# Two stages reordered in a hybrid encoder kernel: low parts behind the next modulation and h made twice by ScalarE; mask squares earlier, one small operation fewer a row, sample keys behind the masks

## Chip, cores and metric

The kernel runs on one core of one Trainium2 chip. The metric is the device time in microseconds (us) of one launch; the time before is the median of three runs. TensorE (PE) multiplies, VectorE (DVE), ScalarE (ACT) and GpSimd (POOL) work beside it, and SyncE (SP) issues the loads. All five run their own instruction lists and wait for each other by semaphores.

## What is computed

One inference step of a two-layer encoder trunk, width 1024, on 1024 prompt positions and 64 sample positions, all in float32. Each layer is `x += gate(c) * mixer(RMSNorm(x) * (1 + scale(c)) + shift(c))`. What the change touches is all in layer 0:

```python
rel = jax.nn.relu(jnp.einsum('bqhd,bsd->bqhs', qi, ki)).astype(jnp.float32)
score = jnp.einsum('bqh,bqhs->bqs', wi.astype(jnp.float32), rel)
adm = (kpos[None, :] // CHUNK) <= (qpos[:, None] // CHUNK)
score = jnp.where(adm[None], score, -jnp.inf)
top_val, top_idx = lax.top_k(score, topk)          # 256 keys of each query
...
logits = jnp.einsum('bqgrd,bqkgd->bqgrk', q, kg).astype(jnp.float32) * (HEAD_DIM ** -0.5)
logits = jnp.where(valid[:, :, None, None, :], logits, -jnp.inf)
p = jax.nn.softmax(logits, axis=-1).astype(v.dtype)
```

The mixer of layer 0 is this sparse attention beside a short gated convolution, both fed from one projection `h @ w_in`; layer 1 is a gated spatial unit. The sample positions attend to 512 cached keys beside their own 64.

## The kernel before

**Products.** A float32 product is made of three fast ones: an operand is split into a high part and a low part (the operand less its high part), and TensorE adds high by high, low by high and high by low. `ah` and `al` are the parts of the activations, `w_hi` and `w_lo` those of a weight tile. The high part is made by ScalarE; the low part by a subtraction on GpSimd (weights, line 253) or on VectorE.

**First stage (`startup`, lines 296 to 418).** The eight tiles of `x` (128 x 1088, one for each 128 of the width, called k-tiles, `kt`) are loaded and their squares summed. Modulation comes in four units `u`; each gives scale and shift of two k-tiles: 32 narrow matmuls (`ada_steps`, line 165), a VectorE copy of their sum (`ada_rows`, line 168), a TensorE transpose (line 171), and two or three small VectorE operations that write `mod` and `modA`. Then, for each k-tile, `scale(kt)` multiplies x by the root-mean-square factor on VectorE (line 339); `h(kt)` makes `hf`, the modulated tile in full float32, on GpSimd (line 345), the same values rounded to the high part `ah` on ScalarE (line 346), and `al = hf - ah` on VectorE (line 347); `part(kt)` issues the matmuls of that k-tile for the first two weight tiles (line 334): six with `ah, w_hi`, six with `ah, w_lo`, six with `al, w_hi`. There are two buffers for `hf`. The order of TensorE, VectorE, GpSimd and ScalarE in this stage is the order of the code: for u = 1 to 3 the modulation's matmuls, the first six matmuls of `part(2u-1)`, the transpose, the other twelve, then `scale` and `h` of the next two k-tiles, then all of `part(2u)`. The last two k-tiles are multiplied for one weight tile after the other. The common products of the later stages (line 261) follow.

**Masks (`masks`, lines 609 to 643).** A search finds for each query the threshold `T` of its 256th score. For each of seven rows of widths 384, 512, 640, 768, 896, 1024 and 576 the kernel then writes a 0/1 mask in which ties are broken by position: ScalarE makes the sign of score less threshold with its sum (line 632) and the square of that with its sum (line 622); VectorE makes a one-column number out of the two sums in two operations (lines 638 and 639), a running count along the row that starts from it (line 640), and a comparison (line 641); ScalarE then scales the mask into a bias (line 643). A sign operation of row j waits in the order for the square of row j-2 (`issue_after`). Here TensorE alone follows the order of the code; the lists of the other engines are set by the framework's planner, which places each instruction when its inputs are due.

**Around the masks.** While the masks are made, TensorE works through `side` steps, the matmuls of two more projections (line 278; 360 steps stand ahead of the attention, the masks are issued at step 289), and their sums are moved out by ScalarE (`q<-pj`). `sample_keys` loads the cached keys (`ckr`), splits them into `kc` (high on ScalarE, line 292; low on GpSimd, line 293) and copies 64 columns of `kp` behind them (line 782); `both_parts` makes the sample queries `qs` (lines 768 and 769). Both are issued ahead of the masks' order here: `sample_keys` before the side steps, `both_parts` at the start of `attend`. The attention begins with logits on TensorE (line 680), each read from its PSUM bank by a VectorE reduction (line 681) and then passed to ScalarE for the exponential. The second pair of logits has to wait until the reduction of an earlier one has freed its bank.

## Time and profile before

| what | us |
| --- | --- |
| runs | 1121.41 (median), 1119.2 to 1122.15 |
| the profiled execution | 1120.84 |
| its span, from the first instruction to the last | 1119.0 |
| TensorE busy in the span | 1080.0 (97%) |
| VectorE, ScalarE, GpSimd busy | 651.7, 524.2, 459.9 |

The profile is of one execution. Its page gives sums over the whole span; the trace gives each instruction with its start and length, and what ended the idle time before it. In the time-ordered view a row that stands for several instructions (x6) begins with the first and its length goes to the end of the last. In the view by stretches a row gives the ends of the stretch, its length, the busy time of TensorE, of its weight loads, of VectorE, ScalarE and GpSimd, then TensorE's granted clock as a share of full speed, the share of the DMA engines that was busy, and GB/s.

### The profile page before, as it was taken

Reading aid. Unit: us, or ns where it says so; the run is one execution under the profiler, and the core shown is the slowest. Engines: PE = TensorE matmul, PEld = TensorE weight load, DVE = VectorE, ACT = ScalarE, POOL = GpSimd, SP = SyncE. Lnnn points to the kernel's source line nnn. Section 1 sums busy time; section 2 is a strip of 40 time slices with the busy share of each in tenths; the row PEclk is TensorE's granted clock in tenths of the full one; section 3 lists DMA queues with packets and bytes.
Section 4 is the critical chain, followed back from the end, with each engine's and each line's share of the span. In section 5 each row is a group of like instructions: output and inputs, shape, how many; then the busy total and the mean of one; then the engine's idle time right before and its main releaser. Section 6 shows DMA issues by size and latency. Waiting matters only on the chain.

```text
span 1119.0 us, 18850 instructions
## 1 busy us (share of the span) xinstructions
PE 1080.0 (97%) x7255; PEld 1044.9 (93%) x7255; DVE 651.7 (58%) x1621; ACT 524.2 (47%) x1003; POOL 459.9 (41%) x479
## 2 busy tenths in 40 slices
PE   5899999999999979999999999999999999999996
PEld 4789778999999979999999999999999999999996
DVE  4710789998887687777786344311393083346134
ACT  5333588766776677667686234411221111244111
POOL 2634224346675625545375356411242101264222
PEclk9999999999999989999999999999999999999999
DMA  9754611211010210000002601111113101130012
GB/s 371 279 198 161 246 30 47 84 42 47 30 39 23 73 38 21 20 18 19 5 22 80 246 1 39 33 44 38 39 48 94 39 20 39 38 132 20 1 67 94
DMA packets 25786, 81.84 MB, mean 73 GB/s; under 512 B 3040, under 2 KB 9440, under 8 KB 23264
## 3 DMA queue, kind: packets, MB, share of 16 engines
q1 hardware_dynamic: 25696, 80.63, 20.5%
q8 instruction: 57, 0.93, 0.3%
q14 instruction: 33, 0.27, 0.1%
HBM read 74.50 MB, written 6.12 MB: 72 GB/s over the span
## 4 chain that ended last, share of the span: by engine, by line
PE 58%; DVE 2%; issue 1%; POOL 1%; ACT 1%; DMA 1%; POOLq 0%; DVEq 0%; ACTq 0%
PE pj L261 24%; PE op L261 15%; PE pj L278 7%; PE av L724 3%; PE logit_ps L680 3%; PE p_ps L706 3%; PE sgu_ps L1204 1%; DVE al L293 1%; DMA w_raw<-in_wo 1%; PE v_ps L1251 1%; POOL w_lo L253 1%; PE op L1123 0%; PE rstd L226 0%; PE sgus_ps L1207 0%; DVE x L1176 0%
## 5 line engine op out<-in xcount | busy, mean ns | idle before, releaser
L261 PE MATMUL pj<-ah,w_hi 128*128 128x364 f32 (+1 forms) x984 | 326.0, 331 | 1.0 <-ACT w_hi L252 1.0
L261 PE MATMUL pj<-al,w_hi 128*128 128x364 f32 (+1 forms) x984 | 323.8, 329 | 0.0
L261 PE MATMUL pj<-ah,w_lo 128*128 128x364 f32 (+1 forms) x984 | 323.0, 329 | 0.0
L253 POOL TENSOR_TENSOR w_lo<-w_raw,w_hi 128x1024 fp32r<-128x1024 f32 x63 | 155.7, 2472 | 322.1 <-ACT w_hi L252 319.8
L261 PEld LDWEIGHTS pj<-ah,w_hi 128*128 128x128 f32 x984 | 185.0, 188 | 2.0 <-ACT w_hi L252 1.3
L261 PEld LDWEIGHTS pj<-ah,w_lo 128*128 128x128 f32 x984 | 184.8, 188 | 0.3 <-issue 0.2
L261 PEld LDWEIGHTS pj<-al,w_hi 128*128 128x128 f32 x984 | 185.1, 188 | 0.0
L252 ACT ACTIVATE w_hi<-w_raw 128x1024 fp32r<-128x1024 f32 x68 | 71.8, 1057 | 107.8 <-PE pj L261 86.6
L545 DVE TENSOR_SCALAR_CACHE_REDUCE junk<-S,cand 128x512 bf16<-128x512 f32 (+5 forms) x142 | 119.0, 838 | 1.9
L261 PE MATMUL op<-al,w_hi 128*128 128x256 f32 (+2 forms) x344 | 112.0, 326 | 0.4 <-DVE al L293 0.4
L261 PE MATMUL op<-ah,w_hi 128*128 128x256 f32 (+2 forms) x344 | 112.2, 327 | 0.0
L261 PE MATMUL op<-ah,w_lo 128*128 128x256 f32 (+2 forms) x344 | 111.6, 326 | 0.0
L278 PE MATMUL pj<-ah,w_hi 128*128 128x364 f32 (+1 forms) x288 | 95.7, 332 | 0.0
L278 PE MATMUL pj<-ah,w_lo 128*128 128x364 f32 (+1 forms) x288 | 95.6, 332 | 0.0
L278 PE MATMUL pj<-al,w_hi 128*128 128x364 f32 (+1 forms) x288 | 95.4, 331 | 0.0
L572 ACT ACTIVATE junk<-S,cand 128x896 bf16<-128x896 f32 (+2 forms) x78 | 77.7, 996 | 29.2 <-DVE m L575 25.5
L1144 DVE SCALAR_TENSOR_TENSOR x<-op,mod,x 128x192 f32<-128x192 f32 (+2 forms) x64 | 30.2, 496 | 101.6 <-PE op L261 97.5
L687 POOL TENSOR_SCALAR S<-S,sm 128x128 f32<-128x128 f32 (+8 forms) x68 | 51.6, 763 | 73.2 <-DVE sm L686 60.5
L1152 POOL TENSOR_TENSOR acc<-acc,sq 128x448 f32<-128x448 f32 (+2 forms) x40 | 40.7, 1018 | 86.3 <-ACT sq L1150 85.5
L261 PEld LDWEIGHTS op<-al,w_hi 128*128 128x128 f32 x344 | 64.9, 189 | 2.5 <-DVE al L293 0.7
L1150 ACT ACTIVATE sq<-x 128x448 f32<-128x448 f32 (+2 forms) x42 | 21.3, 506 | 96.7 <-DVE x L1144 93.2
L261 PEld LDWEIGHTS op<-ah,w_hi 128*128 128x128 f32 x344 | 64.9, 189 | 1.7
(255 smaller groups left out, 2096.9 us busy)
## 6 DMA issues: line engine op xcount, KB each, us to landing
w_raw<-in_w SPq DMA_DIRECT2D x53, 512.0 KB, 3.4
ada<-in_ada_w SPq DMA_DIRECT2D x19, 1024.0 KB, 7.5
w_raw<-in_wo SPq DMA_DIRECT2D x16, 512.0 KB, 3.5
x<-in_x SPq DMA_DIRECT2D x8, 544.0 KB, 5.7
bo<-in_ada_w SPq DMA_DIRECT2D x4, 1024.0 KB, 6.8
x<-in_x SPq DMA_DIRECT2D x1, 1792.0 KB, 7.9
out_y<-x SPq DMA_DIRECT2D x1, 1792.0 KB, 6.6
x<-in_x SPq DMA_DIRECT2D x1, 1536.0 KB, 9.4
```

What stands on the lines that cost most here:

```text
L252: nc.scalar.activation(hi, raw, AF.Copy)
L253: (nc.gpsimd if lo_eng == "pool" else nc.vector).tensor_sub(lo, raw, hi)
L261: last = self.nc.tensor.matmul(ps, wt[:, kt, :], at[:, kt, c0:c1], start=n == 0, stop=n == len(mms) - 1)
L278: self.nc.tensor.matmul(ps, wt[:, kt, :], at[:, kt, a:b], start=kt == 0 and i == 0, stop=kt == KT - 1 and i == 2)
L545: V.tensor_scalar(junks[0][:, 0:SW[j]], self.S[:, span(j)], thr, 0.0, op0=OP.is_lt, op1=OP.add, accum_out=col(cv, j))
L572: nc.scalar.activation(junks[1][:, 0:SW[j]], self.S[:, span(j)], AF.Sign, scale=-1.0, bias=col(cand, j), accum_out=col(cv, j))
L680: nc.tensor.matmul(pt[:, 0:w], lhs, keys[i][:, t // 2, s], start=i == 0, stop=i == 1)
L687: self.lastnorm = nc.gpsimd.tensor_scalar(p, p, st[:, 3:4], 0.5, op0=OP.mult, op1=OP.mult).ins
L706: nc.tensor.transpose(pt[0:r, o:o + P], p[:, j * P:j * P + r], self.ident)
L724: self.lastav = nc.tensor.matmul(av[:, 0:m], self.vs[0:r, vbase + j, t // 2, :], part[0:r, x:x + m], start=j == 0 and i == 0, stop=(j + 1) ...
L1144: nc.vector.scalar_tensor_tensor(x[:, t, a:b], ps[:, a:b], self.mod[l][:, 16 + t, j:j + 1], x[:, t, a:b], op0=OP.mult, op1=OP.add)
L1152: nc.gpsimd.tensor_add(acc, acc, sq)
```

## The change

Three things are edited.

- In `startup`, `part` can issue one of its three kinds of matmuls alone. The `al, w_hi` matmuls of k-tile 2u-2 are issued behind the modulation transpose of unit u, and those of 2u-1 after them. `h` takes two k-tiles at once; `hf` is now made by ScalarE too, from the same inputs as `ah` (four more activations for two k-tiles, 16 in all, and as many fewer GpSimd operations). `scale(kt + 2)` stands ahead of the subtraction of `kt`.
- In `masks`, the square of row 0 comes ahead of the sign of row 1. One VectorE operation makes `(sum of signs - 0.5) * sum of squares` in place of two, and it is used by the comparison; the running count starts from the constant `kneg` and needs only the squares.
- `sample_keys` and `both_parts` are issued after the last square of the masks, and some tiles share other buffers.

```diff
@@ startup @@
-        def part(kt, ns=(0, 1), between=()):
-            for i, (wi, at) in enumerate(((0, self.ah), (1, self.ah), (0, self.al))):
-                if i == 1:
-                    for _ in between:
-                        pass
+        def part(kt, ns=(0, 1), which=(0, 1, 2)):
+            for i in which:
+                wi, at = ((0, self.ah), (1, self.ah), (0, self.al))[i]
...
-        def h(kt):
-            hf = sp.tile([P, TC], F32, tag="hf0", name="hf0", bufs=2)
-            for j, (a, b) in enumerate(((0, SEQ), (SEQ, TC))):
-                sc, sh = self.modA[0][:, kt, j:j + 1], self.mod[0][:, kt, j:j + 1]
-                nc.gpsimd.tensor_scalar(hf[:, a:b], x[kt][:, a:b], sc, sh, op0=OP.mult, op1=OP.add)
-                nc.scalar.activation(self.ah[:, kt, a:b], x[kt][:, a:b], AF.Identity, scale=sc, bias=sh)
-            nc.vector.tensor_sub(self.al[:, kt, :], hf, self.ah[:, kt, :])
+        def h(kts):
+            hfs = []
+            for kt in kts:
+                hfs.append(sp.tile([P, TC], F32, tag="hf0", name="hf0", bufs=2))
+                for out in (self.ah[:, kt, :], hfs[-1]):
+                    for j, (a, b) in enumerate(((0, SEQ), (SEQ, TC))):
+                        nc.scalar.activation(out[:, a:b], x[kt][:, a:b], AF.Identity, scale=self.modA[0][:, kt, j:j + 1],
+                                             bias=self.mod[0][:, kt, j:j + 1])
+            for kt, hf in zip(kts, hfs):
+                if kt + 2 < KT:
+                    scale(kt + 2)
+                nc.vector.tensor_sub(self.al[:, kt, :], hf, self.ah[:, kt, :])
...
             scale(1)
-            h(0)
-            scale(2)
-            h(1)
-            part(0)
+            h((0, 1))
+            part(0, which=(0, 1))
             w_split(0, 2, KT, nc.gpsimd)
             w_split(1, 2, KT, nc.vector)
-            scale(3)
...
-                part(2 * u - 1, between=steps)
-                for kt in (2 * u, 2 * u + 1):
-                    if kt + 2 < KT:
-                        scale(kt + 2)
-                    h(kt)
+                part(2 * u - 1, which=(0,))
+                for _ in steps:
+                    pass
+                part(2 * u - 1, which=(1,))
+                part(2 * u - 2, which=(2,))
+                h((2 * u, 2 * u + 1))
+                part(2 * u - 1, which=(2,))
                 if u < 3:
-                    part(2 * u)
+                    part(2 * u, which=(0, 1))
@@ masks @@
-            pool.tile([P, 2 * 512], BF, tag=t, name="cum", bufs=3) for t in ("ptl", "ptl", "ptl", "pth", "pth")]
+            pool.tile([P, 2 * 512], BF, tag=t, name="cum", bufs=3) for t in ("ptl", "pth", "pth", "pth", "ptl")]
...
-            with self.tc.issue_after(square) if j > 1 else nullcontext():
+            with self.tc.issue_after(square) if j else nullcontext():
                 A.activation(bi, sl, AF.Sign, scale=self.sgn[:, p], bias=self.T[:, p], accum_out=sums[:, 0:1])
-            if j:
-                square = squares(*rows[j - 1])
-        squares(*rows[-1])
+            if j != 1:
+                square = squares(*rows[j - (j > 0)])
+        self.masked = squares(*rows[-1])
         for n, bi, cum, p, sums in rows:
-            c = self.cv[:, p]
-            V.tensor_add(c, sums[:, 0:1], sums[:, 1:2])
-            V.tensor_scalar(c, c, 0.5, self.kneg[:, p], op0=OP.mult, op1=OP.add)
-            V.tensor_tensor_scan(cum, self.ones.to_broadcast([P, n]), cum, c, OP.add, OP.subtract)
-            V.scalar_tensor_tensor(bi, cum, 0.0, bi, op0=OP.is_gt, op1=OP.is_gt)
+            V.tensor_scalar(sums[:, 2:3], sums[:, 0:1], sums[:, 1:2], -0.5, op0=OP.add, op1=OP.mult)
+            V.tensor_tensor_scan(cum, self.ones.to_broadcast([P, n]), cum, self.kneg[:, p], OP.add, OP.subtract)
+            V.scalar_tensor_tensor(bi, cum, sums[:, 2:3], bi, op0=OP.is_gt, op1=OP.is_gt)
@@ sample_keys, attend and the calls @@
-            raw = pool.tile([P, PAST], F32, tag="pth", name="ckr", bufs=3)
+            raw = pool.tile([P, PAST], F32, tag="ptl", name="ckr", bufs=3)
...
-        for t in range(2):
-            self.both_parts(pool, t)
...
                     self.queries(ap, 0)
-                    self.sample_keys(ap)
                     for n in range(BEFORE):
                         if n == MASKS:
                             self.masks(ap)
+                            with self.tc.issue_after(self.masked):
+                                self.sample_keys(ap)
+                                for t in range(2):
+                                    self.both_parts(ap, t)
                         next(self.side)
```

The instruction lists show what this moves. In the first stage, ScalarE before, from the first k-tile's `ah` to the weights' high parts (line, operation, output<-inputs with buffer numbers, shape):

```order
L346 ACTIVATE ah_64<-x0_98,mod0_87,modA0_89 128x1024
L346 ACTIVATE ah_64<-x0_98,mod0_87,modA0_89 128x64
L346 ACTIVATE ah_64<-x1_99,mod0_87,modA0_89 128x1024
L346 ACTIVATE ah_64<-x1_99,mod0_87,modA0_89 128x64
L386 ACTIVATE w_hi_235<-w_raw_123 128x768
L386 ACTIVATE w_hi_237<-w_raw_124 128x768
```

And the same place on ScalarE after the change:

```order
L347 ACTIVATE ah_64<-x0_98,mod0_87,modA0_89 128x1024
L347 ACTIVATE ah_64<-x0_98,mod0_87,modA0_89 128x64
L347 ACTIVATE hf0_273<-x0_98,mod0_87,modA0_89 128x1024
L347 ACTIVATE hf0_273<-x0_98,mod0_87,modA0_89 128x64
L347 ACTIVATE ah_64<-x1_99,mod0_87,modA0_89 128x1024
L347 ACTIVATE ah_64<-x1_99,mod0_87,modA0_89 128x64
L347 ACTIVATE hf0_278<-x1_99,mod0_87,modA0_89 128x1024
L347 ACTIVATE hf0_278<-x1_99,mod0_87,modA0_89 128x64
L391 ACTIVATE w_hi_235<-w_raw_123 128x768
L391 ACTIVATE w_hi_237<-w_raw_124 128x768
```

Four activations of `hf` now stand ahead of the weights' high parts and between the two `ah`. VectorE in the same stretch, from the scaling of k-tile 1 to the modulation copy, before:

```order
L339 TENSOR_TENSOR x1_99<-x1_99,acc0_138 128x1088
L347 TENSOR_TENSOR al_65<-hf0_273,ah_64 128x1088
L339 TENSOR_TENSOR x2_100<-x2_100,acc0_138 128x1088
L347 TENSOR_TENSOR al_65<-hf0_280,ah_64 128x1088
L387 TENSOR_TENSOR w_lo_238<-w_raw_124,w_hi_237 128x768
L339 TENSOR_TENSOR x3_101<-x3_101,acc0_138 128x1088
L168 COPY ada_rows_342<-ada_ps_309 128x128
```

VectorE there after the change:

```order
L338 TENSOR_TENSOR x1_99<-x1_99,acc0_138 128x1088
L338 TENSOR_TENSOR x2_100<-x2_100,acc0_138 128x1088
L352 TENSOR_TENSOR al_65<-hf0_273,ah_64 128x1088
L338 TENSOR_TENSOR x3_101<-x3_101,acc0_138 128x1088
L352 TENSOR_TENSOR al_65<-hf0_278,ah_64 128x1088
L392 TENSOR_TENSOR w_lo_238<-w_raw_124,w_hi_237 128x768
L168 COPY ada_rows_336<-ada_ps_303 128x128
```

The scaling of x moved ahead of the subtractions; the copy `ada_rows`, for which TensorE's transpose waits, still stands behind both subtractions and the weights' low part. On TensorE the six `al, w_hi` matmuls of k-tile 0 left their place ahead of the modulation's matmuls for one behind the transpose, and likewise for k-tiles 2 and 4.

At the masks, ScalarE before, from the first sign to the first square and one further:

```order
L632 ACTIVATE bias,sums<-S,T,sgn 128x384
L252 ACTIVATE w_hi<-w_raw 128x1024
L894 ACTIVATE q<-pj 128x360
L632 ACTIVATE bias,sums<-S,T,sgn 128x512
L768 ACTIVATE qs<-q 64x64 x2
L292 ACTIVATE kc_3878<-ckr 128x512 x2
L622 ACTIVATE cum,sums<-bias 128x384
```

After the change, ScalarE from the first sign:

```order
L637 ACTIVATE bias,sums<-S,T,sgn 128x384
L252 ACTIVATE w_hi<-w_raw 128x1024
L896 ACTIVATE q<-pj 128x360
L627 ACTIVATE cum,sums<-bias 128x384
L637 ACTIVATE bias,sums<-S,T,sgn 128x512
L637 ACTIVATE bias,sums<-S,T,sgn 128x640
```

The first square moved up past a sign, the `qs` pair and the two `kc`. VectorE at the end of the masks before (the running count of line 640 is printed here as SCALAR_TENSOR_TENSOR, in the trace as TENSOR_TENSOR_SCAN; the logits' reduction, line 681, as ISA):

```order
L640 SCALAR_TENSOR_TENSOR cum<-ones,cv,cum 128x1024
L638 TENSOR_TENSOR cv<-sums 128x1
L641 SCALAR_TENSOR_TENSOR bias<-cum,bias 128x1024
L639 TENSOR_SCALAR cv<-cv,kneg 128x1
L681 ISA S,sm<-logit_ps,corner 128x128
L681 ISA sm 128x1
L640 SCALAR_TENSOR_TENSOR cum<-ones,cv,cum 128x576
```

After the change, from the small operation of the 1024 row to the first reduction:

```order
L643 TENSOR_SCALAR sums<-sums 128x1
L644 SCALAR_TENSOR_TENSOR cum<-ones,kneg,cum 128x1024
L643 TENSOR_SCALAR sums<-sums 128x1
L644 SCALAR_TENSOR_TENSOR cum<-ones,kneg,cum 128x576
L645 SCALAR_TENSOR_TENSOR bias<-cum,sums,bias 128x1024
L645 SCALAR_TENSOR_TENSOR bias<-cum,sums,bias 128x576
L685 ISA S,sm<-logit_ps,corner 128x128
L685 ISA sm 128x1
```

Before, the reduction that frees TensorE's bank stood ahead of the count and the comparison of the 576 row; now it stands behind them. GpSimd over the masks before, where `st`, `qs` and `kc` are low parts of queries and keys:

```order
L601 MEMSET cv 128x1 x4
L769 TENSOR_TENSOR st<-q,st 64x512 x4
L253 TENSOR_TENSOR w_lo<-w_raw,w_hi 128x1024
L769 TENSOR_TENSOR qs<-q,qs 64x64 x2
L293 TENSOR_TENSOR kc_3879<-ckr,kc_3878 128x512 x2
L769 TENSOR_TENSOR qs<-q,qs 64x64 x2
L253 TENSOR_TENSOR w_lo<-w_raw,w_hi 128x1024
```

GpSimd there after the change:

```order
L606 MEMSET cv 128x1 x4
L773 TENSOR_TENSOR st<-q,st 64x512 x4
L253 TENSOR_TENSOR w_lo<-w_raw,w_hi 128x1024 x2
L773 TENSOR_TENSOR qs<-q,qs 64x64 x3
L293 TENSOR_TENSOR kc_3881<-ckr,kc_3880 128x512 x2
L773 TENSOR_TENSOR qs<-q,qs 64x64
L253 TENSOR_TENSOR w_lo<-w_raw,w_hi 128x1024
```

The `qs` and `kc` subtractions moved behind the second weight tile's low part. On ScalarE the high parts that they wait for stand behind the last square, and the two `kc<-ckr` behind the scaling of the 896 row (line 647). On SyncE the load of a third weight tile stands ahead of the two loads of `ckr`.

## Rows read from the trace of the kernel before

**Rows 1.** Stretches: the first stage, and masks' end to 586 us.

```profile
core 0: us, PE busy (x) PEld busy (x) DVE busy (x) ACT busy (x) POOL busy (x), PEclk, DMA share, GB/s
27.57:66.69 39.12, 33.41 (x340) 30.42 (x340) 25.70 (x27) 14.62 (x22) 24.71 (x18) 0.96 0.67 248
412.60:586.00 173.40, 172.74 (x1181) 168.45 (x1182) 132.05 (x423) 129.40 (x286) 91.57 (x96) 0.99 0.06 19
```

**Rows 2.** TensorE's waits, 400 to 420 us: total, times, longest.

```profile
PE logit_ps L680 <- DVE sm L681: 6.3, 1, 6.3
```

**Rows 3.** TensorE in time order, first stage; in brackets the idle time before.

```profile
37.90 0.33 PE L171 MATMUL ada_ps<-ident,ada_rows 128*128 128x128 f32 x1 [3.29 <-DVE ada_rows L168]
...
47.66 0.27 PE L171 MATMUL ada_ps<-ident,ada_rows 128*128 128x128 f32 x1
...
56.62 0.27 PE L171 MATMUL ada_ps<-ident,ada_rows 128*128 128x128 f32 x1
...
61.50 0.76 PE L334 MATMUL first<-al,w_hi 128*128 128x364 f32 x3 [1.53 <-DVE al L347]
```

**Rows 4.** Stretches behind TensorE's three longest waits; the clock is the 0.50 or 1.00.

```profile
38.36:41.76 3.40, 3.40 (x14) 3.40 (x13) 1.88 (x5) 3.03 (x4) 2.89 (x3) 0.50 1.02 412
61.50:66.69 5.19, 5.19 (x30) 5.05 (x31) 1.29 (x1) 2.28 (x5) 1.47 (x2) 1.00 0.77 272
412.60:417.23 4.63, 4.61 (x17) 4.61 (x18) 2.73 (x8) 3.96 (x9) 0.73 (x2) 0.50 0.25 97
```

**Rows 5.** ScalarE and GpSimd in time order, first stage.

```profile
26.27 3.04 ACT L346 ACTIVATE ah<-x,mod,modA 128x1024 fp32r<-128x1024 f32 x4 [1.82 <-DVE modA L182]
29.22 1.56 ACT L386 ACTIVATE w_hi<-w_raw 128x768 fp32r<-128x768 f32 x2
...
32.59 1.84 POOL L387 TENSOR_TENSOR w_lo<-w_raw,w_hi 128x768 fp32r<-128x768 f32 x1
```

**Rows 6.** VectorE in time order, first stage.

```profile
32.65 2.92 DVE L347 TENSOR_TENSOR al<-hf,ah 128x1088 fp32r<-128x1088 f32 x1 [0.30 <-POOL hf L345]
35.50 0.95 DVE L387 TENSOR_TENSOR w_lo<-w_raw,w_hi 128x768 fp32r<-128x768 f32 x1
...
37.57 0.28 DVE L168 COPY ada_rows<-ada_ps 128x128 f32<-128x128 f32 x1
...
61.74 1.29 DVE L347 TENSOR_TENSOR al<-hf,ah 128x1088 fp32r<-128x1088 f32 x1 [0.30 <-POOL hf L345]
```

**Rows 7.** ScalarE in time order, start of the masks.

```profile
385.45 0.80 ACT L632 ACTIVATE bias<-S,T,sgn 128x512 bf16<-128x512 f32 x1
...
387.85 0.51 ACT L622 ACTIVATE cum<-bias 128x384 bf16<-128x384 bf16 x1
```

**Rows 8.** VectorE in time order, masks.

```profile
394.62 0.15 DVE L638 TENSOR_TENSOR cv<-sums 128x1 f32<-128x1 f32 x1
...
395.06 1.55 DVE L640 TENSOR_TENSOR_SCAN cum<-ones,cv,cum 128x640 bf16<-128x640 f32 x1
...
397.82 3.85 DVE L640 TENSOR_TENSOR_SCAN cum<-ones,cv,cum 128x768 bf16<-128x768 f32 x1
...
412.29 0.28 DVE L681 CUSTOM_DVE_ANT_0 S<-logit_ps,corner 128x128 f32<-128x128 f32 x1
```

**Rows 9.** VectorE's groups by form, 383 to 415 us: busy, mean ns, idle.

```profile
L640 DVE TENSOR_TENSOR_SCAN cum<-ones,cv,cum 128x512 bf16<-128x512 f32 x1 | 1.3, 1287 | 0.0
L641 DVE SCALAR_TENSOR_TENSOR bias<-cum,bias 128x1024 bf16<-128x1024 bf16 x1 | 1.2, 1212 | 0.0
...
L641 DVE SCALAR_TENSOR_TENSOR bias<-cum,bias 128x512 bf16<-128x512 bf16 x1 | 0.7, 694 | 0.0
```

**Rows 10.** GpSimd in time order, masks.

```profile
385.32 2.40 POOL L253 TENSOR_TENSOR w_lo<-w_raw,w_hi 128x1024 fp32r<-128x1024 f32 x1 [0.58 <-POOL st L769]
387.80 0.71 POOL L769 TENSOR_TENSOR qs<-q,qs 64x64 fp32r<-64x64 f32 x2
388.59 3.20 POOL L293 TENSOR_TENSOR kc<-ckr,kc 128x512 fp32r<-128x512 f32 x2
```

More of the change, by code (lines that the diff above doesn't have):

```diff
@@ L1002, in layer0 @@
                 ap.tile([P, TC], F32, tag="ga", name="place")
+                ap.tile([P, 512], F32R, tag="pth", name="place", bufs=3)
+                st = ap.tile([P, 2 * SEQ], F32R, tag="sta", name="st")
+                self.st = [[st[:, e * SEQ:(e + 1) * SEQ] for e in range(2)]]
                 self.kc = [ap.tile([P, 2 * NS], F32R, tag=f"kc{i}", name=f"kc{i}").rearrange("p (g n) -> p g n", g=2)
                            for i in range(2)]
-                st = ap.tile([P, 2 * SEQ], F32R, tag="sta", name="st")
-                self.st = [[st[:, e * SEQ:(e + 1) * SEQ] for e in range(2)]]
                 def gate_b(t):
```

## The prediction

> **What bounds the kernel now.** I read the stretches first, to see where TensorE is not the bound. From the masks' end to 586 us it is busy 172.74 of 173.40 us, but in the first stage only 33.41 of 39.12 us [rows 1]: 5.7 us idle or between matmuls. TensorE's waits come next. Around the masks there is one, 6.3 us, for VectorE's first logits reduction, which frees a bank [rows 2]; TensorE went dry at 406.3 and resumed at 412.6. In the first stage the longest are 3.29 us for the modulation copy `ada_rows` and 1.53 us for the low part of k-tile 6 [rows 3]. Third, the clock: behind the waits of 3.29 and 6.3 us TensorE worked 3.4 and 4.6 us at 0.50, the lower of its two levels (1.2 GHz), while it stayed at 1.00 (2.4 GHz) behind the 1.53 us [rows 4]. Work at half clock loses half its length, so these stretches lost 1.7 and 2.3 us. Everywhere else TensorE is full, and the change touches no matmul there. So only two places can pay, each bounded by its waits and its half-clock stretch.
>
> **One property of VectorE and GpSimd** is needed in both places. The subtraction `al` takes 1.29 us by itself, but 2.92 us where GpSimd's `w_lo` had begun at 32.59, 0.06 us before it, and ran 1.84 us [rows 5, 6]. At the masks, the running count takes 1.29 us for 512 columns and 1.55 for 640 [rows 8, 9], 0.26 for each 128, so 1.82 for 768; the trace has 3.85 [rows 8], 2.03 more, and a weight's low part (2.40 us each [rows 10]) ran on GpSimd there. VectorE operations on two SBUF tiles wait out a GpSimd operation that began first.
>
> **First stage, step by step.** ScalarE makes both `ah` of a pair in 3.04 us [rows 5], 0.76 each; with the two `hf` a pair takes 6.1, less a little overlap, 6.0. I count to the three transposes (37.90, 47.66, 56.62) and to the end at 66.69 [rows 1, 3].
> To the first: ScalarE's pair from 26.27 ends at 32.25 and `al` of k-tile 1 at 33.6. The first `w_hi` takes 0.78 [rows 5] and is done at 33.05, so GpSimd's `w_lo` follows `al` at 33.5 and ends at 35.3; VectorE's own `w_lo` waits for that and takes 0.95, to 36.1 [rows 6]; the copy takes 0.28. Transpose at 36.36, 1.54 earlier. TensorE lost the six `al` matmuls ahead of it, so the wait stays at about 3.4 us, and I keep the half-clock stretch behind it.
> First to second: TensorE has the same six groups of matmuls and the modulation; it was bound by itself (9.76) and stays so, 9.66.
> Second to third: 8.96 before, of which 0.45 was a wait for a low part that is no longer needed there: 8.5. ScalarE's chain would allow 0.78 + 6.0 + 1.33 + 0.28 = 8.4, so the two are level.
> Third to end: 10.07 before. Now `hf` of k-tile 7 ends 0.78 + 6.0 after the transpose, its `al` takes 1.33 with its start [rows 6], and seven of the last twelve half-groups (3.6 us, from 5.19 for ten [rows 4]) are left: 11.7. That is 1.6 longer, since ScalarE now makes four tiles in turn where two engines made two each.
> Sum 36.36 + 9.66 + 8.5 + 11.7 = 66.2: **0.5 us gained**. Bounds: 1.5 if the last k-tile's wait is shared with matmuls I count twice; a loss of 0.3 if the second and third stretch fall to ScalarE's pace.
>
> **Masks, step by step.** VectorE's chain began when the first square (0.51 us from 387.85) was in. That square now takes the place of the second sign, at 385.45 [rows 7], so the chain starts at 386.1 in place of 388.5: 2.4 earlier.
> Its own work: counts of 4800 columns in seven rows, 11.5 us at 0.25 + 0.26 for each 128; comparisons 0.69 for 512 and 1.21 for 1024 [rows 9], so 0.17 + 0.13 for each 128, 6.1; small operations, two of which took 0.44 (394.62 to 395.06 [rows 8]), now one at about 0.15, 1.0. Together 18.6, so 404.7 without a stall. Before, the first reduction ran at 412.29 [rows 8] and stood ahead of the 576 row's count and comparison; now it stands behind them, 1.41 + 0.75 us of the 18.6.
> Stalls by GpSimd: the first `w_lo` runs from 385.32 to 387.72 [rows 10], 1.5 on the chain. The second falls on a comparison, 2.0 to 2.4. The `kc` and `qs` subtractions no longer fall at the start. By ScalarE's list they follow the last square and, for `kc`, the scaling of the 896 row, around 403 to 404; the three `qs` ahead of them on GpSimd take 0.36 each [rows 10] and get between VectorE's last operations one at a time, 1.1 or less. I take 4.7 of stalls: 386.1 + 18.6 + 4.7 = 409.4, **2.9 us gained**, and a TensorE wait of 3.4 us.
> Bounds: 4.5 gained if the `qs` fall behind the chain and the second `w_lo` costs 1.6; 0.5 if both `kc` (3.20 with their own stalls [rows 10], 2.4 without) get in as well.
> Who waits for what moves back: ScalarE's `q` evacuations and `kc` stand later, but TensorE's side steps have five matmuls between logits, and the sample logits are not among the first, so I cost these at nothing; without that cover TensorE would wait once for a bank, and the 6.3 us [rows 2] is what such a wait can reach.
>
> **The clock.** A wait of 3.4 us at the masks is next to the 3.29 that dropped the clock, so I keep half clock there, but for 3.4 us as behind 3.29 and not 4.6 [rows 4]: **0.6 gained**.
>
> **Sum.** 0.5 + 2.9 + 0.6 = 4.0 from the profiled execution's 1120.84: 1116.8. The median, 1121.41, is 0.57 above that execution, which would give 1117.4. I forecast **1117.1**, itself from 1115.7 to 1118.6.
>
> **Rivals.**
> (1) The clock stays full at the masks. With stalls of 3.1 only, the chain ends at 407.8 and TensorE waits 1.8 us, near the 1.53 that kept 1.00. Gain 0.5 + 4.5 + 2.3 = 7.3: 1114. For it: only one of the `w_lo` has to miss by a little. Against: the wait has to shrink by two thirds.
> (2) The `kc` subtractions get between VectorE's last operations. ScalarE's list puts their inputs at 404, and three `qs` on GpSimd are all that holds them back from a chain that ends at 409. 1.2 to 2.4 more: 1118.3 to 1119.8, say 1119. Then the change moves a stall from the masks' start to their end, and does not do what it says.
> (3) Slower. If every GpSimd subtraction falls whole on the chain, the stalls are 1.5 + 2.4 + 2.4 (three `w_lo`), 3.2 (`kc`) and 1.4 (four `qs`), 10.9: 386.1 + 18.6 + 10.9 = 415.6, 3.3 later than before, less the first stage's 0.5: 1124. It decides from stalls of 7.6 on (412.3 less 404.7). Against it: before, the same subtractions were on the chain and cost 5.3 (23.8 from 388.5 to 412.29, less 18.5 of its own: 18.6 with two operations more a row and without the 576 row).
> The Trainium skill bears on this rival: "SBUF — State Buffer", section "SBUF: two separate sides", says that a port pair is locked by VectorE (with two SBUF inputs) or GpSimd, whichever starts first, for the whole instruction, and the other blocks fully. By that rule the trace agrees (3.85 for 1.82). It speaks against this change in so far as GpSimd work is moved next to the end of the chain, where the rule would charge all of it.
> (4) The first stage, with ScalarE alone, gives nothing or loses 0.3, the masks as in the forecast: 1118.
>
> **Chances.** Forecast 0.48; clock full 0.20; `kc` in between 0.20; slower 0.06; first stage nothing 0.06. The range of 8 in 10 reaches from 1113.5 to 1119.6, over (1) and (2). About 0.3%, 3.4 us, is what a measurement of this kernel can tell from no change, so faster is below 1118.0. The forecast's upper end, (2) and (4) lie at or above that: faster 0.68, same 0.26, slower 0.06.
>
> **What would show it.** The first transpose after the change near 36.4, 12 more us of ScalarE in the first stage (four pairs of 3.0), and TensorE's last wait there for the low part of k-tile 7. At the masks: the first square at 385 (earlier by the first stage's 0.5), the first reduction at 409, TensorE's wait 3.4 us, and behind it the clock at 0.50. GpSimd's `kc` after the first reduction would confirm the forecast against (2); a granted clock of 1.00 there is (1). Wrong would be a first stage that ends after 67, or a new wait of TensorE in the attention.

## The result

The changed kernel takes **1114.53 us** (median of 7 runs, 1113.11 to 1117.74); the kernel before, run beside it, 1120.59 (median of 7, 1119.06 to 1122.15). The ratio is **0.9950** with an interval of 0.9934 to 0.9966, so the change is worth 6 us, between 3.8 and 7.4. The forecast was 1117.1 with a range of 1113.5 to 1119.6.

The stretches of the profiled execution after the change (columns as in [rows 1]): the first stage, then the stretch at half clock behind the wait for the first transpose, then the one behind the wait at the masks.

```profile
26.25:64.71 38.46, 32.94 (x339) 30.40 (x340) 21.60 (x27) 26.36 (x38) 3.44 (x2) 0.96 0.70 269
34.99:38.08 3.09, 3.08 (x11) 3.09 (x12) 1.60 (x4) 2.11 (x3) 0.00 (x0) 0.50 0.99 387
406.86:410.14 3.28, 3.28 (x12) 3.28 (x13) 0.73 (x4) 3.16 (x9) 3.12 (x3) 0.50 0.00 0
```

The first stage takes 38.46 us where it took 39.12 [rows 1]; behind the masks' wait TensorE works 3.3 us at half clock where it was 4.6 [rows 4]. TensorE's waits after the change (total, times, longest), to be held against [rows 2, 3]:

```profile
PE ada_ps L171 <- DVE ada_rows L168: 4.0, 2, 3.4
PE logit_ps L684 <- DVE sm L685: 2.8, 1, 2.8
...
PE first L333 <- DVE al L352: 2.1, 2, 1.2
```

The wait at the masks fell from 6.3 to 2.8 us. The transposes and the end of the first stage, and the first matmul behind the masks' wait, in TensorE's order of time:

```profile
34.99 0.48 PE L171 MATMUL ada_ps<-ident,ada_rows 128*128 128x128 f32 x1 [3.41 <-DVE ada_rows L168]
...
44.60 0.27 PE L171 MATMUL ada_ps<-ident,ada_rows 128*128 128x128 f32 x1
...
52.93 0.33 PE L171 MATMUL ada_ps<-ident,ada_rows 128*128 128x128 f32 x1
...
61.11 0.77 PE L333 MATMUL first<-al,w_hi 128*128 128x364 f32 x3 [1.17 <-DVE al L352]
...
64.71 0.33 PE L261 MATMUL pj<-ah,w_hi 128*128 128x364 f32 x1
...
406.86 0.69 PE L684 MATMUL logit_ps<-kp,st 128*128 128x128 f32 x2 [2.77 <-DVE sm L685]
```

VectorE's chain at the masks, its start, the three places where GpSimd stalls it, and the reduction that ends it:

```profile
383.88 0.21 DVE L643 TENSOR_SCALAR sums<-sums 128x1 f32<-128x1 f32 x1 [2.68 <-ACT cum L627]
384.01 2.32 DVE L644 TENSOR_TENSOR_SCAN cum<-ones,kneg,cum 128x384 bf16<-128x384 f32 x1
...
396.64 3.12 DVE L645 SCALAR_TENSOR_TENSOR bias<-cum,sums,bias 128x896 bf16<-128x896 bf16 x1
...
403.57 3.02 DVE L645 SCALAR_TENSOR_TENSOR bias<-cum,sums,bias 128x1024 bf16<-128x1024 bf16 x2
406.51 0.28 DVE L685 CUSTOM_DVE_ANT_0 S<-logit_ps,corner 128x128 f32<-128x128 f32 x1
```

GpSimd over the same time; each of those three rows has its partner here:

```profile
383.12 2.39 POOL L253 TENSOR_TENSOR w_lo<-w_raw,w_hi 128x1024 fp32r<-128x1024 f32 x1 [0.58 <-POOL st L773]
396.16 2.65 POOL L253 TENSOR_TENSOR w_lo<-w_raw,w_hi 128x1024 fp32r<-128x1024 f32 x1 [10.65 <-ACT w_hi L252]
399.75 4.02 POOL L773 TENSOR_TENSOR qs<-q,qs 64x64 fp32r<-64x64 f32 x3 [0.94 <-ACT qs L772]
403.85 3.87 POOL L293 TENSOR_TENSOR kc<-ckr,kc 128x512 fp32r<-128x512 f32 x2
...
408.19 2.38 POOL L253 TENSOR_TENSOR w_lo<-w_raw,w_hi 128x1024 fp32r<-128x1024 f32 x1
```

The two executions differ by 6.2 us, in these pieces (first product, hand-over to line 261, first sign of the masks, first logits, resumption, end): 1.3 ahead of the first product, 0.66 in the first stage, 0.2 up to the masks, 3.56 in the masks' wait, 0.4 behind it. The 1.3 us stands ahead of every changed instruction. Kernel before:

```profile
18.10:23.30 5.20, 5.20 (x65) 4.63 (x65) 1.08 (x5) 0.95 (x2) 2.52 (x3) 0.81 1.05 409
```

And after:

```profile
18.10:23.30 5.20, 5.20 (x92) 4.56 (x90) 1.63 (x7) 1.60 (x5) 2.53 (x4) 1.00 1.05 407
```

The same code ran partly at half clock in one execution and not in the other. Of the experiments below, two with the changed first stage (first alone, square second) have it too, and their first product is at 28.2 us; in the others it is at 25.55 to 27.11. It comes and goes with the execution and is no part of the change, so about 5 of the 6.2 us between these two executions belong to the edits.

### The profile page after: what moved, and what is told of

Its sections match the earlier page's. It is cut to its first block, busy times and chain, and to the rows that moved or that the text cites. A ratio compares the mean times of both kernels' runs of the same rounds, so it can differ in the third digit from the quotient of the medians.

```text
span 1112.8 us, 18831 instructions
## 1 busy us (share of the span) xinstructions
PE 1077.3 (97%) x7255; PEld 1042.8 (94%) x7255; DVE 645.6 (58%) x1614; ACT 535.4 (48%) x1019; POOL 440.9 (40%) x463
## 4 chain that ended last, share of the span: by engine, by line
PE 88%; DVE 6%; ACT 4%; issue 2%; DMA 0%; POOL 0%; POOLq 0%; DVEq 0%; ACTq 0%
PE pj L261 44%; PE op L261 15%; PE pj L278 9%; PE av L728 3%; PE logit_ps L684 3%; PE p_ps L710 3%; PE ada_ps L165 2%; PE first L333 2%; PE sgu_ps L1210 1%; PE score_ps L448 1%; DVE cum L644 1%; PE score_ps L449 1%; DVE al L293 1%; ACT rel L451 1%; DVE bias L645 1%
```

## The experiments

All compute the whole result. Ratios are to the kernel before, measured beside them on the same chip. Experiments are set against each other by these ratios.

**First stage alone.** The kernel before with all of `startup` as changed.

```diff
-        def part(kt, ns=(0, 1), between=()):
+        def part(kt, ns=(0, 1), which=(0, 1, 2)):
...
-        def h(kt):
+        def h(kts):
```

> The first stage as changed, the masks and the sample keys as before. Theory (each part pays for itself): the stretch from the first product to the hand-over shrinks from 39.1 to 38.5 us, the 6.3 us wait at the masks stays; 0.5 to 1.0 us faster than before. Rival (the 1.3 us by which the changed kernel's first product began earlier belong to the change of this stage): about 2 us faster, with the clock at 1.00 between 20 and 23 us in this run and 0.5 to 0.6 in the kernel before.

Measured 1119.68 us, ratio 1.0000 (0.9991 to 1.0008): nothing. Each step of the stage is as in the changed kernel but one, the stretch from the first transpose to the second, 10.7 us in place of 9.6:

```profile
35.69:42.51 6.82, 5.55 (x19) 5.55 (x20) 4.31 (x8) 4.58 (x7) 0.20 (x1) 0.50 0.84 322
```

The wait ahead of it:

```profile
36.96 0.47 PE L171 MATMUL ada_ps<-ident,ada_rows 128*128 128x128 f32 x1 [3.40 <-DVE ada_rows L168]
```

The clock fell within the wait of 3.40 us and stayed at 0.50 for 6.8 us; TensorE worked 5.55 us of them, against 3.1 in the changed kernel's profile behind 3.41. Over its 11 runs the granted clock of the whole span is 0.991 on average, that of the 23 runs of the kernel before 0.993; 0.002 of 1118 us is 2 us (an upper bound, since half clock in a wait costs nothing), more than the stage's gain. Runs of equal clock bear this out, though they are few: at 0.993 two runs of this kernel took 1118.2 us on average and 17 of the kernel before 1119.9, at 0.991 four took 1119.7 and two 1121.7. So the stage is shorter, and the lower clock takes it back: the theory that the part pays for itself falls, and so does the rival, since the 1.3 us are not there.

**Masks and keys alone.** The changed kernel with all of `startup` as before.

```diff
-        def part(kt, ns=(0, 1), which=(0, 1, 2)):
+        def part(kt, ns=(0, 1), between=()):
...
-        def h(kts):
+        def h(kt):
```

> The masks and sample keys as changed, the first stage as before. Theory: TensorE's wait before the second logits falls from 6.3 to about 2.8 us and the half-clock stretch behind it from 4.6 to about 3.2 us of work, so 4.0 to 4.5 us faster than before; the first stage is 39.1 us. Rival (the two parts only pay together): below 3 us.

Measured 1115.95 us, ratio 0.9965 (0.9952 to 0.9979): 3.9 us, just under the theory's 4.0 to 4.5. TensorE's wait is that of the changed kernel:

```profile
407.51 0.44 PE L679 MATMUL logit_ps<-kp,st 128*128 128x128 f32 x2 [2.78 <-DVE sm L680]
```

But behind it the clock stayed full in the profiled execution, which is 2.4 us below the median:

```profile
407.51:412.00 4.49, 4.49 (x28) 4.49 (x29) 2.21 (x12) 4.16 (x13) 4.33 (x6) 1.00 0.01 2
```

**Keys early.** Both stages as changed, the sample keys and queries (and the buffers that they share) where they were before.

```diff
+        for t in range(2):
+            self.both_parts(pool, t)
...
+                    self.sample_keys(ap)
                     for n in range(BEFORE):
                         if n == MASKS:
                             self.masks(ap)
-                            with self.tc.issue_after(self.masked):
-                                self.sample_keys(ap)
-                                for t in range(2):
-                                    self.both_parts(ap, t)
```

> Both parts of the change, but the sample keys and queries issued where they were before. Theory (GpSimd's kc and qs subtractions stall VectorE wherever they stand): the first square comes 1.7 us later than in the changed kernel, behind the kc and qs activations, the kc stalls come at the start of the chain and not at its end, and the comparison of the 576 row falls behind the first reduction; the wait is 2.8 to 3.6 us and the time within 1 us of the changed kernel. Rival (the move of the keys is what pays): the wait is 5 us or more and the time 2 to 4 us above the changed kernel's.

Measured 1118.52 us, ratio 0.9988 (0.9979 to 0.9997); TensorE's wait is 5.9 us. The theory is wrong and the rival right: 4 us above the changed kernel's ratio. Two rows of VectorE show what the theory had left out:

```profile
389.50 0.21 DVE L643 TENSOR_SCALAR sums<-sums 128x1 f32<-128x1 f32 x1 [1.34 <-ACT cum L627]
...
405.68 3.44 DVE L645 SCALAR_TENSOR_TENSOR bias<-cum,sums,bias 128x1024 bf16<-128x1024 bf16 x1
```

And of GpSimd:

```profile
405.70 2.34 POOL L253 TENSOR_TENSOR w_lo<-w_raw,w_hi 128x1024 fp32r<-128x1024 f32 x1 [6.57 <-ACT w_hi L252]
```

The chain starts 4.25 us behind the first sign (2.65 in the changed kernel, 5.0 before), it waits 1.3 us more for the second square, and it is then late enough for the third weight's low part to fall on its last long comparison. In the changed kernel that `w_lo` stands on GpSimd behind `qs` and `kc` and begins at 408.19, after the first reduction.

**Keys alone.** The kernel before with only the keys moved, and the buffers that they share.

```diff
-        for t in range(2):
-            self.both_parts(pool, t)
...
-                    self.sample_keys(ap)
                     for n in range(BEFORE):
                         if n == MASKS:
                             self.masks(ap)
+                            with self.tc.issue_after(self.masked):
+                                self.sample_keys(ap)
+                                for t in range(2):
+                                    self.both_parts(ap, t)
```

> The kernel before with only the sample keys and queries moved behind the last square; the order of the squares, the two small operations a row and the first stage are as before. Theory (the keys are half of the masks' gain: they held up the first square by 1.6 us, and on GpSimd they now keep the third weight's low part behind VectorE's chain): the wait of 6.3 us falls to 4.5 to 5.5, 1 to 2 us faster than before. Rival (the keys are all of it): the wait is near 2.8 us.

Measured 1119.89 us, ratio 1.0001 (0.9993 to 1.0010). TensorE's waits at the logits:

```profile
PE logit_ps L680 <- DVE sm L681: 5.7, 1, 5.7
...
PE logit_ps L680 <- ACT q L892: 0.7, 1, 0.7
```

The long wait lost 0.6, a new one of 0.7 took it back. The keys are neither half of the gain nor all of it: theory and rival both miss. The end of VectorE's chain shows why the wait is so long:

```profile
407.58 2.18 DVE L640 TENSOR_TENSOR_SCAN cum<-ones,cv,cum 128x576 bf16<-128x576 f32 x1
409.80 0.76 DVE L641 SCALAR_TENSOR_TENSOR bias<-cum,bias 128x576 bf16<-128x576 bf16 x1
410.47 0.28 DVE L681 CUSTOM_DVE_ANT_0 S<-logit_ps,corner 128x128 f32<-128x128 f32 x1
```

The chain starts 1.6 us earlier than before (3.44 us behind the first sign), but the 576 row's two operations, which before stood behind the first reduction, now stand ahead of it, and a `kc` falls on the first of them.

**Two small operations a row.** The changed kernel with lines 638 to 641 of before.

```diff
-            V.tensor_scalar(sums[:, 2:3], sums[:, 0:1], sums[:, 1:2], -0.5, op0=OP.add, op1=OP.mult)
...
+            V.tensor_add(c, sums[:, 0:1], sums[:, 1:2])
+            V.tensor_scalar(c, c, 0.5, self.kneg[:, p], op0=OP.mult, op1=OP.add)
...
```

> The changed kernel with the two small operations a row of before (the count again starts from their result); the squares' order and the keys as changed. Theory (the chain has to be short enough to end before GpSimd's kc subtractions, so that the three parts of the masks' edit pay together and little by themselves): the chain is 1.9 us longer by itself, which puts the second kc subtraction on it as well, so TensorE's wait is 4.8 to 6 us and the time 2 to 4 us above the changed kernel. Rival (each part pays its own size): the wait is 4.5 us at most.

Measured 1119.29 us, ratio 0.9990 (0.9979 to 1.0001); the wait is 5.7 us, in the theory's range, and the ratio 4.5 us above that of the changed kernel, a little more than the theory's 2 to 4. VectorE at three places:

```profile
397.15 2.35 DVE L643 TENSOR_TENSOR cv<-sums 128x1 f32<-128x1 f32 x1
...
405.75 1.15 DVE L643 TENSOR_TENSOR cv<-sums 128x1 f32<-128x1 f32 x1
...
408.20 2.18 DVE L645 TENSOR_TENSOR_SCAN cum<-ones,cv,cum 128x576 bf16<-128x576 f32 x1
```

GpSimd's two `kc`:

```profile
403.65 5.51 POOL L293 TENSOR_TENSOR kc<-ckr,kc 128x512 fp32r<-128x512 f32 x2
```

The chain, 1.9 us longer by itself, is caught by both `kc` (1.0 at 405.75, 0.8 at 408.20); it took 25.7 us from its start to the first reduction, 22.6 in the changed kernel.

**Square second.** The changed kernel with the first square behind the second sign again.

```diff
-            with self.tc.issue_after(square) if j else nullcontext():
+            with self.tc.issue_after(square) if j > 1 else nullcontext():
...
-            if j != 1:
-                square = squares(*rows[j - (j > 0)])
+            if j:
+                square = squares(*rows[j - 1])
```

> The changed kernel with the first row's square behind the second row's sign again. Theory: the chain starts 0.8 us later; TensorE's wait is 3.4 to 4.8 us (the upper end if the kc subtractions follow suit), 0.6 to 2.5 us above the changed kernel. Rival (the square's place is most of the masks' gain): a wait of 5 us or more.

Measured 1116.91 us, ratio 0.9970 (0.9959 to 0.9981); the chain starts 0.79 us later (3.44 us behind the first sign) and the wait is 3.5 us: the lower end of the theory. The ratio is 2.2 us above that of the changed kernel, more than the wait accounts for; the granted clock of its runs is lower too, 0.992 on average against 0.994.

**hf on GpSimd.** The changed kernel with `hf` made as before, the rest of the first stage as changed.

```diff
-                for out in (self.ah[:, kt, :], hfs[-1]):
...
+                    nc.gpsimd.tensor_scalar(hfs[-1][:, a:b], x[kt][:, a:b], sc, sh, op0=OP.mult, op1=OP.add)
```

> The changed kernel with hf made on GpSimd again, the low parts and the scaling of x still moved. Theory (ScalarE's second tile brings the first transpose forward by 1.5 us but the end of the stage back by 1.7 us): the first transpose is 9.5 to 10.3 us behind the first product in place of 8.7, the last stretch 10 us in place of 11.8; the whole stage within 0.7 us of the changed kernel's 38.5. Rival (ScalarE's h is what the gain of the stage rests on): the stage takes 39.5 us or more.

Measured 1115.24 us, ratio 0.9960 (0.9946 to 0.9975), not to be told from the changed kernel. The first and the third transpose and the hand-over; the first product is at 26.47:

```profile
36.69 0.47 PE L171 MATMUL ada_ps<-ident,ada_rows 128*128 128x128 f32 x1 [4.42 <-DVE ada_rows L168]
...
55.57 0.33 PE L171 MATMUL ada_ps<-ident,ada_rows 128*128 128x128 f32 x1 [0.37 <-DVE ada_rows L168]
...
65.81 0.33 PE L261 MATMUL pj<-ah,w_hi 128*128 128x364 f32 x1
```

First transpose 10.2 us behind the first product, last stretch 10.2 us: ScalarE's second tile does bring the one forward and the other back, by 1.5 each way. The stage took 39.3 us, between the theory's upper end (39.2) and the rival's 39.5, with the clock at half for 6.8 us around and behind a wait of 4.4, 4.4 of them work.

**The low part behind the copy.** The changed kernel with one VectorE operation moved.

```diff
-            w_split(1, 2, KT, nc.vector)
+            nc.scalar.activation(ws[1][0][:, 2:KT, :], wraw[1][:, 2:KT, :], AF.Copy)
...
                 for _ in steps:
                     pass
+                if u == 1:
+                    nc.vector.tensor_sub(ws[1][1][:, 2:KT, :], wraw[1][:, 2:KT, :], ws[1][0][:, 2:KT, :])
```

> The changed kernel with one VectorE operation moved: the low part of the second weight tile (0.95 us alone, 2.3 us where GpSimd's own w_lo runs beside it) stands behind the first unit's copy ada_rows and modA, not ahead of them. Theory (the wait of 3.4 us before the first transpose is made by that operation, and it is this wait that draws the half clock in the first stage, so that the part alone gained nothing): the transpose comes 2.2 us earlier, the wait is 1.2 us, the clock stays at 1.00 in the first stage, which takes 35.0 to 35.5 us in place of 37.2 (no half clock) to 39.6; 2.2 to 4 us faster than the changed kernel. Rival (the wait goes over to a low part or the copy itself): the stage stays above 37 us and the time within 1 us.

Measured 1112.54 us, ratio 0.9931 (0.9918 to 0.9944). The first transpose:

```profile
32.13 0.33 PE L171 MATMUL ada_ps<-ident,ada_rows 128*128 128x128 f32 x1 [0.81 <-DVE ada_rows L168]
```

And the stretches behind it and behind the masks' wait, which is 2.8 us here too:

```profile
32.13:41.17 9.04, 8.39 (x101) 7.67 (x101) 7.11 (x9) 5.97 (x8) 1.43 (x1) 1.00 1.02 418
403.44:407.00 3.56, 3.56 (x23) 3.56 (x24) 1.40 (x8) 3.53 (x11) 3.40 (x3) 1.00 0.00 0
```

The operation that was moved, as it stood in the changed kernel beside GpSimd's `w_lo`:

```profile
32.44 2.30 DVE L392 TENSOR_TENSOR w_lo<-w_raw,w_hi 128x768 fp32r<-128x768 f32 x1 [0.17 <-ACT w_hi L391]
```

The wait is 0.8 us, the stage 35.5 us in place of 38.5, the clock full, as it is in the first stage of the three later profiles with this edit. The theory holds for the stage: this one operation made the wait behind which the clock fell in five of the six profiles that have it. The ratio is 2.1 us below that of the changed kernel, just under the theory's 2.2 to 4, and the two intervals overlap.

**Last row behind the logits.** The changed kernel with the 1024 row made last (rows in the order 0, 1, 2, 3, 4, 6, 5; `finish` holds the loops over the rows), its VectorE work behind the sixth reduction.

```diff
+        finish(rows[:-1])
+        self.rest = lambda: finish(rows[-1:])
...
                 self.logits(it, e, c)
+                done += 1
+                if done == 6:
+                    with self.tc.issue_after(self.lastred):
+                        self.rest()
```

> The changed kernel with the row of 1024 columns made last and its VectorE operations behind the sixth logits reduction. Theory (TensorE's wait is the VectorE chain's length and the half clock is the wait's): the chain ends about 3.8 us earlier, the wait is below 0.6 us, the clock stays at 1.00 through the masks; 3 to 4 us faster than the changed kernel, less what the count of 2.35 us costs among the reductions. Rival (another wait takes its place, or the count delays the reductions by as much as it frees): within 1 us of the changed kernel.

Measured 1113.41 us, ratio 0.9941 (0.9930 to 0.9953), about 1 us below the changed kernel, which is no more than the two intervals. TensorE's waits at the logits, the one that went and the one that came:

```profile
402.69 0.44 PE L687 MATMUL logit_ps<-kp,st 128*128 128x128 f32 x2 [0.39 <-DVE sm L688]
...
413.43 0.53 PE L687 MATMUL logit_ps<-kc,qs 128*128 128x288 f32 x2 [1.70 <-DVE sm L688]
```

The wait and the half clock are gone (1.00 up to 1104 us in this execution), but the count costs 1.7 among the reductions: the rival's mechanism, at part of its price. The first reduction comes 2.4 us sooner behind the chain's start, not 3.8, since both `kc` now fall on the two operations of the 576 row. In this execution the first stage had no half clock either, behind a wait of 3.24 us; from the first transpose to the second:

```profile
34.29:42.67 8.38, 8.38 (x101) 7.67 (x101) 5.58 (x8) 5.98 (x8) 0.00 (x0) 1.00 1.03 416
```

**The same row later, with the low part moved.** The last two edits together, the count behind the twelfth reduction (the 1024 row has buffers of its own here).

```diff
-                if done == 6:
+                if done == 12:
```

> The edit of e5 and that of the last row together, the count of the 1024 row now behind the twelfth logits reduction, where TensorE has more side steps ready, in place of the sixth. Theory (both waits are gone and the clock is full from the first product to the attention): TensorE waits at most 0.5 us at the logits, no half clock before 1100 us, 5 to 7 us faster than the changed kernel, near 1108.5. Rival (the count holds up the reductions there too): a wait of 1 to 2 us behind the twelfth reduction, near 1110.5.

Measured 1109.62 us, ratio 0.9917 (0.9903 to 0.9930). VectorE at the row's two long operations:

```profile
415.30 2.34 DVE L647 TENSOR_TENSOR_SCAN cum<-ones,kneg,cum 128x1024 bf16<-128x1024 f32 x1
...
419.20 1.28 DVE L648 SCALAR_TENSOR_TENSOR bias<-cum,sums,bias 128x1024 bf16<-128x1024 bf16 x1
```

And TensorE:

```profile
421.24 0.63 PE L716 MATMUL p_ps<-ident,S 128*128 128x128 f32 x4 [2.29 <-DVE ptl L293]
```

The theory is right on the clock in this execution (0.39 us of wait at the second logits, 1.00 up to 1102 us), though two of the five runs have clocks of 0.994 and 0.995. The rival is right on the row: TensorE waits 2.3 us there for the low part of the probabilities, which stands behind the comparison.

**Last pair on GpSimd.** The low part moved, and `hf` of k-tiles 6 and 7 on GpSimd.

```diff
+                        if kt >= KT - 2 and out is hfs[-1]:
+                            nc.gpsimd.tensor_scalar(out[:, a:b], x[kt][:, a:b], sc, sh, op0=OP.mult, op1=OP.add)
```

> The edit of e5 with hf of the last pair on GpSimd. Theory (with ScalarE alone the last low part is what the stage ends on; before, two engines shared it): the stretch from the third transpose to the hand-over is 10.0 to 10.3 us in place of 11.8, the stage 33.7 us; 1.5 us faster than e5. Rival (GpSimd's operations and the subtractions block each other): 11 us or more.

Measured 1110.46 us, ratio 0.9913 (0.9898 to 0.9928). The third transpose and the hand-over, the first product being at 27.11:

```profile
50.83 0.33 PE L171 MATMUL ada_ps<-ident,ada_rows 128*128 128x128 f32 x1
...
61.06 0.33 PE L261 MATMUL pj<-ah,w_hi 128*128 128x364 f32 x1
```

The last stretch is 10.23 us in place of 11.77, the stage 33.95, close to the theory's 33.7; the ratio is 2 us below that of the low part alone, and the two intervals overlap.

**All of it, with the 640 row.** The edit above, and the 640 row last and behind the sixteenth reduction, with buffers of its own.

```diff
-        for k, j in enumerate((0, 1, 2, 3, 4, 6, 5)):
+        for k, j in enumerate((0, 1, 3, 4, 5, 6, 2)):
...
-                if done == 12:
+                if done == 16:
```

> The edit of e5, hf of the last pair on GpSimd as before, and the 640 row (the last that the attention needs) made last, its count behind the sixteenth reduction. Theory: the first stage is 33.7 us (the last stretch 10.1 in place of 11.8), TensorE's wait before the second logits is below 0.8 us, no half clock before 1100 us, and the count of 1.55 us costs at most 1 us among the reductions: near 1107. Rival (a count among the reductions costs what it saves ahead of them): a wait of 1.5 us or more behind the sixteenth reduction and no gain over e5 with the last pair on GpSimd.

Measured **1107.46 us**, ratio **0.9883** (0.9868 to 0.9898), the fastest of all. TensorE's waits at the attention:

```profile
400.10 0.44 PE L693 MATMUL logit_ps<-kp,st 128*128 128x128 f32 x2 [1.22 <-DVE sm L694]
...
422.89 0.63 PE L719 MATMUL p_ps<-ident,S 128*128 128x128 f32 x4 [1.24 <-DVE ptl L293]
```

The two waits are 1.2 us each, more than the 0.8 and 1 that the theory had, and the clock is full to 1098 us. The kernel is 3 us below the one above, which lacks only the move of the 640 row (1110.46, measured beside it), and every run of the one is below every run of the other: the rival falls.

## Why the prediction came out as it did

**First stage: the steps held, their worth did not.** From the first product to the first transpose the forecast had 8.8 us (36.36 less 27.57) and the profile has 8.74; to the second 9.66 and 9.61; to the third 8.5 and 8.33; to the end 11.7 and 11.78. The sum, 38.6, is 38.46 in the trace. (The printed terms of the first step add to 36.5 and not to 36.36, with which the 8.8 is worked out.) Yet alone the part gives nothing (1.0000), and the changed kernel's ratio is no further below that of the masks alone than the two intervals allow. The step that failed is the sentence "so the wait stays at about 3.4 us, and I keep the half-clock stretch behind it": the wait did stay (3.41), but what it draws is not fixed. In six profiles with this wait (3.2 to 3.4 us) the clock was at half for 6.8 us four times (first alone, keys early, two small operations, square second; 5.6 to 5.9 us of it work), for 3.4 once (the changed kernel; 3.1 of it work) and not at all once (last row); the stretch between the transposes is then 10.7 to 10.9, 9.6 and 8.4 us. In the three profiles with the old stage (before, masks alone, keys alone) it was 3.4 each time. So 0.5 us of gain stood against 1.2 us or so that comes or goes with the clock, and rival (4), that the first stage gives nothing, is what this part did by itself. Why the longer half clock is more frequent with the changed stage is not settled. The length of the wait alone is not it: keys early has 6.8 us behind 3.19, a shorter wait than the old stage's 3.28 to 3.29. Less work stands ahead of the wait, but no run varied that alone.

**Masks: the mechanism held, the sum was 0.7 us too cautious.** The chain started 2.65 us behind the first sign, forecast 2.66 (386.1 less 383.44). Its length to the first reduction is 22.6 us (383.88 to 406.51), forecast 23.3: stalls of 1.3 at the 384 row's count, 2.0 at the 896 row's comparison and 1.1 at the last two comparisons are 4.4, forecast 4.7, and its own work is 18.2, forecast 18.6. The three `qs` cost next to nothing, since they slipped in between VectorE's long operations; one `kc` did get in, ahead of the first reduction. So the stalls came out near the forecast partly by luck: the 1.1 us that it gave to the `qs` was paid to a `kc`, which is rival (2)'s mechanism at the lower end of its price, and the sign that the forecast had set against (2), `kc` behind the first reduction, held for one of the two. The wait is 2.77, forecast 3.4, and the gain 3.56, forecast 2.9.

**But the credit was given to the wrong edits.** I wrote that the square "takes the place of the second sign" and put the whole 2.4 us of earlier start on that. The square's place is worth 0.8 (square second); the other 1.6 come from the `qs` and `kc` activations that the keys' move takes out of its way (keys early starts at 4.25). Nor do the parts add up. Without the keys' move the wait is 5.9, without the merged operation 5.7, with the keys alone 5.7, with everything 2.8, against 6.3 before. The chain has to end before GpSimd's next pieces are due: late by 1.6 to 1.9 us (keys early, two small operations), it is caught by the third `w_lo` or by both `kc`, and TensorE's wait grows by 3, so 1.0 to 1.5 more than the lateness. This is rival (2)'s mechanism, which I had as a fate of the whole change; it is what befalls the chain when the keys' move or the merge is missing. In keys early part of the rest is a second wait for a square (1.3 us). What I did not ask is how near the chain's end stood to GpSimd's next operation.

**The clock at the masks.** The forecast kept half clock for 3.4 us, and the profile has 3.3. But behind the same wait of 2.8 us it stayed at 1.00 in two other profiles (masks alone, low part behind the copy) and fell in two more (hf on GpSimd, last pair on GpSimd), so rival (1) happens in a part of the executions, at this wait and not at the 1.8 us that I had worked it out for. That is one reason why the runs lie between 1113.1 and 1117.7, with granted clocks from 0.996 to 0.992.

**Why the median lies 2.6 us below the forecast.** It is not that the clock stayed full: the median run is the profiled execution, in which the clock fell at the masks as forecast. The masks' wait gave 0.7 us more than forecast and the first stage 0.2. The largest piece, 1.3 us, lies ahead of the first product and is chance: the execution that the forecast started from had the half clock there, at a granted clock of 0.991, while 48 of the 60 runs of that kernel beside the experiments had 0.993 or more (the 42 at 0.993 took 1119.8 us on average).

**The rest.** Rival (3), slower by whole-length stalls, did not occur: 4.4 us of GpSimd's work fell on the chain and not 10.9. The rule that I had set beside it, in the Trainium skill's page "SBUF — State Buffer", section "SBUF: two separate sides", still agrees with the stalls shown: the first to start runs to its end (`w_lo` 2.39 us at 383.12) and the other waits (2.32 for a count that takes 1.02 in two small operations). One row is too close to tell: in keys early the comparison that waited is printed as starting at 405.68, the `w_lo` that held it up at 405.70. What the rule alone does not give is the order in which they start, and here that order decided.

## What to carry to other kernels

When a chain on one engine shares a lock with another, work out where the other's next operations stand at the chain's new end, not only how much shorter the chain gets: the keys' move gave nothing alone, the two other edits 1.3 us without it (with the changed first stage, which by itself gives nothing), and all three 3.9. A wait of about 3 us on TensorE costs more than its length, and not the same in each execution, so look for the one operation that makes it (here a subtraction of 0.95 us that nobody needed yet; moving it took 3 us off the stage in the profile, and about 2 us off the runs, within their intervals) before shaving the stage around it. Moving a producer from two engines to one brought the first transpose forward by 1.5 us here and put the end of the stage back by as much, where nothing is left to hide it.

## What the runs showed of the hardware

- **The same wait, three outcomes.** Around and behind 3.2 to 3.4 us of idling TensorE's clock stayed at 1.00 or fell to 0.50 for 3.4 or 6.8 us, and at 2.8 us it fell in three profiles and not in two. The Trainium skill ("TensorE: Matmul & The Clock Gate", section "Part 1: The HAM clock gate (the "warmup" mystery)") says of a kernel's start that the number of slow matmuls varies from run to run, because the activity monitor runs free of the kernel. These profiles show such a variation behind a wait inside the kernel; that it has the same cause is not shown.
- **A one-column operation can take 2.35 us.** `TENSOR_TENSOR` on two columns of 128x1, 0.15 us by itself [rows 8], took 2.35 behind GpSimd's `w_lo` (two small operations, 397.15). The merged `TENSOR_SCALAR`, whose second number is a per-partition scalar, took 0.21 at 383.88 while a `w_lo` was running (383.12 to 385.51): it was not held up at all. The stall was not saved, though: it fell on the count behind it (2.32 us for 1.02).
